# Loading the first two products' weights in units of 1, 1, 2 and 4 tiles, with the x tiles between them, and eight warm-up products in place of ten

## The chip, the cores and the metric

The kernel runs on one core of one Trainium2 chip. The metric is the device time of one execution in microseconds (us). The kernel before takes 1129.25 us, the median of three runs (1127.74 to 1129.56). One further execution was profiled, and all rows below are of that one.

## The reference

`reference()` takes an activation `x` of 512 positions by 1024 channels in fp32 through two blocks. The first has a gated linear recurrence layer ("layer a") and a sliding-window attention layer ("layer b"); the second has two attentions side by side and a squared-ReLU MLP of 4096. What matters here is how it begins:

```python
h = rmsnorm(x, norm_g)                  # a row of 1024 divided by its root mean square, times g
u = h @ w_in                            # 1024 x 3072
xb, gate = u[..., :1536], u[..., 1536:]
xb = causal_depthwise_conv(xb, conv_w, conv_b)
...                                     # r, i: sigmoids of block products of xb; a, b from them
_, hs = lax.associative_scan(_linear_combine, (a, b), axis=1)
y = hs * silu(gate)
return x + y @ w_out                    # 1536 x 1024
```

## The kernel before, in words

Everything is held transposed: channels on the 128 partitions, the 512 positions along the free axis. `x` is 8 tiles of 128x512 (256 KB each), a weight matrix is cut into tiles of 128x128 (64 KB each). One output tile of `h @ w_in` is 128 channels by 512 positions and sums over 8 pairs of a weight tile and an x tile.

fp32 accuracy is reached with three products for each such pair. An operand is split into a high part, rounded to the type fp32r, and a low part, the difference; the products are high*high, high*low and low*high (`mm3`, L443). So each weight that is loaded is first rounded (`hi_task`, L491: an ACT, DVE or POOL instruction) and then subtracted (`lo_task`, L505: always DVE), and each x tile is multiplied by its norm weight and rounded on ACT, and subtracted on DVE (`split`, L647). The division by the root mean square is put off: it is applied when an output leaves PSUM, so the first products don't wait for the norm, only the first evacuations do (`wait_norm`, called in `xb_evac`, L777).

Weights arrive in units, listed in `plan` in the order in which the products use them. A unit is usually 8 tiles (512 KB). The first two outputs are computed together by `gemm_pair` (L580): for each segment of the sum, one unit of output 0 and one of output 1 are taken, and the two outputs' products alternate along k, so that each x tile is used for six products when it comes. In the kernel before a segment there has 4 tiles, so the pair has four units of 256 KB.

Three tasks handle units: `raw_task` (L479) issues the DMA, `hi_task` rounds, `lo_task` subtracts. `raw_task` may run ahead by `RAW_MAX` = 6 widths of 512 columns. `pieces` (L474) says in how many instructions a unit is rounded and subtracted: the first unit in pieces of 128 columns, others whole. `x_load(j)` (L1716) issues the DMA of x tile j; tile 0 follows the small tensor `vec` (93 KB, norm weights and biases), and tile j > 0 waits until more than (j + 1) // 2 units have been issued. All DMAs go through one queue, SP's.

The order of all instructions is not written out by hand. A planner (`Sched`, L100) holds the tasks as generators, keeps a clock for each engine with its own costs, and each time picks the task with the lowest priority number among those that can start within a window on an engine; an operation that may run on several engines goes to the one where it would finish first. It draws random priorities from seeds; for each of four stages of the network eight seeds are tried in the planner and the one with the earliest planned end is taken (`_orders`, L1877). The instructions of the whole kernel come out of this, so a change at the start can reorder what lies behind it. In the rounding step units with an index below 8 may go to ACT or DVE (`also="copy"`), those from 8 on to ACT or POOL (`also="pool"`).

Before the first real product, `WARM` products of a zeroed bf16 tile (L1731) run on PE.

Layer a ends with `a_w_out`: its first four outputs are computed over the gated tiles y_a[0] to y_a[7] first and over y_a[8] to y_a[11] later (`gemm_open`, L605). DVE makes the low part of each y_a tile as the last step of a chain of gate, scan and product (`rg_post`, `ga_evac`).

Of the kernel before, what the change touches and what calls it, by code (L numbers as in the profile page):

```python
# [16 lines left out]
P = 128  # L17
T = 512
# [9 lines left out]
NSM = 48  # L28
RAW_MAX = 6
LOOK = 6  # L30
WARM = 10
MAXU = 6
WINDOW = 40.0
SLACK = 800.0
# [241 lines left out]
def kernel(ctx: ExitStack, tc: tile.TileContext, io: dict, out: bass.AP, seeds=(0,), trial=False):  # L276
# [12 lines left out]
    fa = Slots(NS_F)  # L289
# [21 lines left out]
    def f_(i):  # L311
        return FB[:, i, :]

    def p_(i):
        return PS[:, i, :]
# [105 lines left out]
    def MMS(lst):  # L421


        def emit():
            for o, l, r, st, sp, _ in lst:
                nc.tensor.matmul(out=o, lhsT=l, rhs=r, start=st, stop=sp)  # L426

        dur = 0.0
        rd, wr = [], []
        seen = set()  # L430
        for o, l, r, _, _, c in lst:
            dur += c
            for lst2, ap in ((rd, l), (rd, r), (wr, o)):
                k = (ap.name, ap.offset, tuple(ap.shape))
                if k not in seen:
                    seen.add(k)
                    lst2.append(ap)
        return Op([("PE", dur, emit, None)], rd, wr)
# [4 lines left out]
    def mm3(o, wh, wl, xh, xl, start, stop):  # L443
        c = cost(_free(o))
        return [(o, wh, xh, start, False, c), (o, wh, xl, False, False, c), (o, wl, xh, False, stop, c)]
# [8 lines left out]
    def DMA(o, i):  # L454
        n = _free(o) * o.shape[0] * 4
        return Op([("SP", n / 360.0, lambda: nc.sync.dma_start(out=o, in_=i), None)], [i], [o])  # L456
# [6 lines left out]
    pos = {"u": 0, "s": 0, "r": 0}  # L463

    def wide(i):
        return (plan[i].shape[-1] + T - 1) // T

    def span(a, e):
        return sum(wide(i) for i in range(a, e))
# [3 lines left out]

    def pieces(i):  # L474
        n = plan[i].shape[-1]
        st = P if i == 0 else 2 * T
        return [(c, min(c + st, n)) for c in range(0, n, st)]

    def raw_task():  # L479
        for i in range(len(plan)):  # L480
            w = wide(i)
            yield lambda: i <= pos["s"] or (span(pos["s"], i + 1) <= RAW_MAX and (i < pos["s"] + 2 or fa.room() >= 6))
            s = yield from fa.get(w)
            n = plan[i].shape[-1]
            yield DMA(FBW[:, s * T:s * T + n], plan[i])
            raws[i] = s
            pos["r"] = i + 1
# [3 lines left out]
    def hi_task():  # L491
        for i in range(len(plan)):
            w = wide(i)
            yield lambda: i in raws and (
                i <= pos["u"] or span(pos["u"], i + 1) <= 2 or (span(pos["u"], i + 1) <= LOOK and ra.room() >= 12)
            )
            s = yield from ra.get(2 * w)
            for c, e in pieces(i):
                yield A(
                    RBW[:, s * T + c:s * T + e], FBW[:, raws[i] * T + c:raws[i] * T + e], AF.Copy,  # L500
                    also="copy" if i < 8 else "pool",
                )
            his[i] = s

    def lo_task():  # L505
        for i in range(len(plan)):
            yield lambda: i in his
            w = wide(i)
            s = his.pop(i)
            for c, e in pieces(i):  # L510
                yield TT(
                    RBW[:, (s + w) * T + c:(s + w) * T + e], FBW[:, raws[i] * T + c:raws[i] * T + e],
                    asf(RBW[:, s * T + c:s * T + e]), ALU.subtract,
                )
            fa.free(raws.pop(i), w)
            units[i] = (s, w)
            pos["s"] = i + 1
# [5 lines left out]
    def need():  # L523
        i = pos["u"]
        pos["u"] += 1
        yield lambda: i in units
        return units.pop(i)

    def wpair(u, c):

        s, w = u
        return RBW[:, s * T + c.start:s * T + c.stop], RBW[:, (s + w) * T + c.start:(s + w) * T + c.stop]

    def wfree(u):
        ra.free(u[0], 2 * u[1])
# [3 lines left out]
    def add(u, fn):  # L539
        plan.extend(u)  # L540
        jobs.append(fn)
# [9 lines left out]
    def ksegs(k0, k1, step=8):  # L551
        return [(k, min(k + step, k1)) for k in range(k0, k1, step)]

    def wsl(w, n, a, b):
        return io[w][n, :, a * P:b * P]

    def have(lst, k):
        return lambda: lst[k] is not None
# [19 lines left out]
        add([wsl(w, n, a, e) for a, e in segs], fn)  # L578

    def gemm_pair(w, n0, n1, kt, acts, evac, prio=3):  # L580
        segs = ksegs(0, kt, 4)

        def fn():
            bs = []
            for n in (n0, n1):
                b = yield from pa.get(1, 1)
                bs.append(b)
            for a, e in segs:
                us = []
                for _ in bs:  # L590
                    u = yield from need()
                    us.append(u)
                for k in range(a, e):
                    yield have(acts, k)
                    c = slice((k - a) * P, (k - a + 1) * P)
                    for b, u in zip(bs, us):
                        yield MMS(mm3(p_(b), *wpair(u, c), *acts[k], k == 0, k == kt - 1))
                for u in us:
                    wfree(u)
            for n, b in zip((n0, n1), bs):  # L600
                S.spawn(evac(n, b), prio)

        add([wsl(w, n, a, e) for a, e in segs for n in (n0, n1)], fn)
# [98 lines left out]
    def x_ready(j, gset, nrm):  # L702
        x = f_(xs[j])
        for g, dst in gset:
            S.spawn(split_act(x, g, dst, j), -1 if nrm is n_a else 1)
        S.spawn(sq_add(nrm, x), 4 if nrm is n_a else 1.5)
# [182 lines left out]
    def layer_a():  # L889
# [4 lines left out]
        def ga(a, e):  # L894
            for j in range(a, e):
                gemm("a_w_in", KR + j, KD, act_a, ga_evac)

        gemm_pair("a_w_in", 0, 1, KD, act_a, xb_evac)
        xb(2, 6)
        ga(0,1)  # L900
# [815 lines left out]
    def x_load(j):  # L1716
        if j == 0:
            yield DMA(vec, io["vec"])
        else:
            yield lambda: pos["r"] > (j + 1) // 2  # L1720
        yield DMA(f_(xs[j]), io["x"][j])
        x_ready(j, [("a_g", act_a)], n_a)

    with tc.manual_schedule():
        nc.vector.memset(warm, 0.0)
        nc.vector.memset(eps, EPS)
        nc.vector.memset(half, -0.5)
        nc.scalar.activation(out=lt[:, 0, 0:1], in_=eps, func=AF.Exp)
        S.table = "exp"
        for j in range(WARM):  # L1730
            nc.tensor.matmul(out=p_(7), lhsT=warm[:, 0:P], rhs=warm, start=True, stop=True)  # L1731
        for j in range(KD):
            S.spawn(x_load(j), 0.1 * j)
        S.spawn(raw_task(), 2.5)
        S.spawn(hi_task(), w_prio)
        S.spawn(lo_task(), w_prio)
        S.spawn(const_task(), 0)
        S.spawn(lam_task(), 4)
        S.spawn(main(), 5)
        try:  # L1740
            S.run()
        except Enough:
            return S.clock["PE"]
# [163 lines left out]
```

## Time and profile before

| | before |
|---|---|
| median of three runs | 1129.25 us |
| the profiled execution's own time | 1129.1 us |
| its span in the profile | 1127.3 us |
| mean granted TensorE clock | 0.996 |
| PE busy | 1115.4 us (99%), 5324 instructions |
| DVE busy | 762.4 us (68%) |
| ACT busy | 404.0 us (36%) |
| POOL busy | 269.2 us (24%) |

PE is TensorE's matmul stream, PEld its weight loads, DVE is VectorE, ACT is ScalarE, POOL is GpSimd, SP is SyncE, whose queue (SPq) issues the DMAs. Times in the rows are microseconds from the start of the span. The 1.8 us between the span and the execution's own time lie around the span. A matmul's end is modelled, so PE counts as busy also where products are spaced wider than they could be; the number of products in a stretch tells more than the busy time there.

### The profile page before, as it was taken

How to read it: one execution, taken by the hardware profiler on the slowest of the kernel's cores; microseconds unless marked ns; L12 is line 12 of the kernel's file. 1: busy time of each engine (PE TensorE's matmuls, PEld its weight loads, DVE VectorE, ACT ScalarE, POOL GpSimd, SP SyncE). 2: the span in 40 equal slices, each digit the busy share in tenths (PEclk: the TensorE clock that was granted, in tenths of full speed). 3: DMA queues.
4: the chain of work that ended last, by engine and by line, in shares of the span. 5: the costliest groups of instructions: out<-in, count | busy, mean ns of one | idle time of the engine just before them, and what ended most of it. 6: DMA issues, size and time to landing. Idle time of an engine off the chain costs nothing.

```text
span 1127.3 us, 14746 instructions
## 1 busy us (share of the span) xinstructions
PE 1115.4 (99%) x5324; PEld 931.0 (83%) x5324; DVE 762.4 (68%) x1349; ACT 404.0 (36%) x823; POOL 269.2 (24%) x353
## 2 busy tenths in 40 slices
PE   9999999999999999999999999999999999999997
PEld 6888888888888878888888888888888888888887
DVE  7999999675797896668676477786653235655332
ACT  5447753334767621177153253111111211111111
POOL 1222242023746521043123124213100002111100
PEclk9999999999999999999999999999999999999998
DMA  7334345306333521712554625423333322233001
GB/s 292 90 113 124 116 131 187 97 16 171 108 92 86 176 80 46 220 54 97 166 167 115 188 91 186 169 94 107 99 94 112 113 75 94 75 93 112 1 1 75
DMA packets 46792, 127.41 MB, mean 113 GB/s; under 512 B 6272, under 2 KB 7936, under 8 KB 46720
## 3 DMA queue, kind: packets, MB, share of 16 engines
q1 hardware_dynamic: 46720, 126.47, 35.8%
q8 instruction: 42, 0.69, 0.3%
q14 instruction: 30, 0.25, 0.1%
HBM read 106.53 MB, written 2.10 MB: 96 GB/s over the span
## 4 chain that ended last, share of the span: by engine, by line
PE 93%; DVE 2%; issue 1%; DMA 1%; SPq 1%; POOL 1%; ACT 1%; POOLq 0%; DVEq 0%; ACTq 0%
PE ps L426 90%; PE ps L450 3%; SPq L456 1%; DMA fb<-in_mk 1%; DMA fb<-in_a_w_in 0%; DVE rb L374 0%; ACT rb L350 0%; DVE fb L374 0%; POOL fb L402 0%; DVE fb L994 0%; POOL col_b L416 0%; DVE fb L405 0%; DVE rb L388 0%; ACT fb L350 0%; DVE fb L388 0%
## 5 line engine op out<-in xcount | busy, mean ns | idle before, releaser
L426 PE MATMUL ps<-rb 128*128 128x512 f32 (+2 forms) x4856 | 1083.6, 382 | 3.0 <-ACT rb L350 2.5
L426 PEld LDWEIGHTS ps<-rb 128*128 128x128 f32 x4856 | 877.2, 188 | 173.6 <-ACT rb L350 3.6
L374 DVE TENSOR_TENSOR rb<-fb,rb 128x1024 fp32r<-128x1024 f32 (+5 forms) x305 | 297.3, 995 | 69.4 <-ACT rb L350 58.0
L359 POOL TENSOR_SCALAR rb<-fb 128x1024 fp32r<-128x1024 f32 (+4 forms) x149 | 156.9, 1062 | 611.6 <-PE ps L426 479.9
L350 ACT ACTIVATE rb<-fb 128x512 fp32r<-128x512 f32 (+4 forms) x149 | 109.2, 741 | 357.1 <-DVE fb L388 164.2
L374 DVE TENSOR_TENSOR fb<-ps,fb 128x512 f32<-128x512 f32 (+3 forms) x142 | 83.5, 590 | 138.4 <-PE ps L426 123.1
L374 DVE TENSOR_TENSOR fb<-fb 128x512 f32<-128x512 f32 (+1 forms) x120 | 88.1, 740 | 23.2 <-ACT rb L350 21.3
L402 POOL TENSOR_SCALAR fb<-fb,sm 128x256 f32<-128x256 f32 (+2 forms) x112 | 64.8, 595 | 118.4 <-DVE sm L419 76.9
L350 ACT ACTIVATE fb<-fb,sm 128x256 f32<-128x256 f32 (+2 forms) x128 | 65.3, 513 | 37.1 <-DVE sm L396 23.2
L388 DVE SCALAR_TENSOR_TENSOR fb<-ps,fb 128x512 f32<-128x512 f32 x56 | 38.5, 687 | 55.4 <-PE ps L426 55.3
L350 ACT ACTIVATE rb<-ps 128x512 fp32r<-128x512 f32 (+2 forms) x86 | 45.3, 537 | 77.3 <-PE ps L450 67.9
L374 DVE TENSOR_TENSOR rb<-ps,rb 128x512 fp32r<-128x512 f32 (+2 forms) x86 | 51.9, 612 | 28.3 <-ACT rb L350 26.6
L350 ACT ACTIVATE fb<-fb 128x512 f32<-128x512 f32 (+1 forms) x63 | 37.5, 611 | 62.0 <-DVE fb L374 54.3
L350 ACT ACTIVATE rb<-fb,vec 128x512 fp32r<-128x512 f32 x41 | 28.5, 719 | 85.3 <-DVE fb L374 74.8
L350 ACT ACTIVATE fb<-ps 64x256 f32<-64x256 f32 (+2 forms) x68 | 30.0, 442 | 63.9 <-PE ps L426 31.5
L450 PE MATMUL ps<-ident,fb 128*128 128x128 f32 x328 | 49.8, 272 | 1.2 <-DVE fb L1593 0.9
L450 PEld LDWEIGHTS ps<-ident,fb 128*128 128x128 f32 x328 | 40.6, 140 | 11.3 <-DVE fb L1593 1.1
L994 DVE CUSTOM_DVE_ANT_0 fb<-ps,fb 128x256 f32<-128x256 f32 (+1 forms) x64 | 28.8, 487 | 11.4 <-PE ps L426 9.5
L388 DVE SCALAR_TENSOR_TENSOR rb<-fb,vec,rb 128x512 fp32r<-128x512 f32 x41 | 30.5, 762 | 0.3
L388 DVE SCALAR_TENSOR_TENSOR fb<-fb,vec 128x512 f32<-128x512 f32 x36 | 29.1, 829 | 0.0
L994 DVE CUSTOM_DVE_ANT_0 fb<-ps,fb,sm_qs 128x256 f32<-128x256 f32 (+1 forms) x64 | 26.3, 442 | 2.7 <-POOL fb L402 1.3
L350 ACT ACTIVATION_READ_ACCUMULATOR fb<-fb,sm 128x1 f32 x128 | 24.1, 189 | 0.0
(90 smaller groups left out, 331.3 us busy)
## 6 DMA issues: line engine op xcount, KB each, us to landing
rb<-rb SPq DMA_DIRECT2D x128, 128.0 KB, 2.3
fb<-in_w_down SPq DMA_DIRECT2D x32, 512.0 KB, 3.7
fb<-in_w_in SPq DMA_DIRECT2D x31, 512.0 KB, 4.1
fb<-in_w_up SPq DMA_DIRECT2D x29, 512.0 KB, 3.5
fb<-in_a_w_in SPq DMA_DIRECT2D x22, 512.0 KB, 4.1
fb<-in_b_w_in SPq DMA_DIRECT2D x16, 512.0 KB, 3.7
fb<-in_mb SPq DMA_DIRECT2D x8, 640.0 KB, 4.6
fb<-in_a_w_out SPq DMA_DIRECT2D x8, 512.0 KB, 3.5
```

The lines of the kernel that those rows point to most:

```text
L350: opts = [("ACT", dur, lambda: nc.scalar.activation(out=o, in_=i, func=fn, **kw), TABLES.get(fn))]
L359: lambda: nc.gpsimd.tensor_scalar(out=o, in0=i, scalar1=1.0, scalar2=1.0, op0=ALU.mult, op1=ALU.mult), None,
L374: lambda: nc.vector.tensor_tensor(out=o, in0=a, in1=b, op=op), None,
L388: lambda: nc.vector.scalar_tensor_tensor(out=o, in0=a, scalar=s, in1=b, op0=op0, op1=op1), None,
L402: ("POOL", 262.0 + 0.832 * n, lambda: nc.gpsimd.tensor_scalar(out=o, in0=a, scalar1=s, scalar2=1.0, op0=ALU.mult, op1=ALU.mult), None),
L426: nc.tensor.matmul(out=o, lhsT=l, rhs=r, start=st, stop=sp)
L450: nc.tensor.transpose(o, i, ident)
L456: return Op([("SP", n / 360.0, lambda: nc.sync.dma_start(out=o, in_=i), None)], [i], [o])
L994: nc.vector.tensor_tensor_reduce(out=pt[h], in0=PS[:, b, o0:o0 + nk], in1=m, scale=sc, scalar=-3.0e38, op0=ALU.add, op1=ALU.max, accum_out ...
```

## The change

Three edits. The pair's segments become 1, 1, 2 and 4 tiles long, which gives eight units (64, 64, 64, 64, 128, 128, 256 and 256 KB) in place of four of 256 KB, each rounded and subtracted in one instruction. The x tiles are issued at other points between the units, and the first ten units may be issued however far `raw_task` is ahead. The number of warm-up products falls from ten to eight.

```diff
-WARM = 10
+WARM = 8
...
     def pieces(i):
         n = plan[i].shape[-1]
-        st = P if i == 0 else 2 * T
-        return [(c, min(c + st, n)) for c in range(0, n, st)]
+        return [(0, n)]
...
-            yield lambda: i <= pos["s"] or (span(pos["s"], i + 1) <= RAW_MAX and (i < pos["s"] + 2 or fa.room() >= 6))
+            yield lambda: i < 10 or i <= pos["s"] or (span(pos["s"], i + 1) <= RAW_MAX and (i < pos["s"] + 2 or fa.room() >= 6))
...
     def gemm_pair(w, n0, n1, kt, acts, evac, prio=3):
-        segs = ksegs(0, kt, 4)
+        segs = [(0, 1), (1, 2), (2, 4), (4, kt)]
...
         else:
-            yield lambda: pos["r"] > (j + 1) // 2
+            yield lambda: pos["r"] >= (0, 2, 4, 6, 6, 8, 8, 8)[j]
         yield DMA(f_(xs[j]), io["x"][j])
```

## Rows read from the trace of the kernel before

**Rows 1.** The page, part 1: busy us, share of the span, instructions of each engine.
```profile
PE 1115.4 (99%) x5324; PEld 931.0 (83%) x5324; DVE 762.4 (68%) x1349; ACT 404.0 (36%) x823; POOL 269.2 (24%) x353
```

**Rows 2.** Timeline of PE, 0 to 60 us: start, us, engine, line, tiles, count.
```profile
1.17 4.35 PE L1731 MATMUL ps<-warm 128*128 128x512 bf16 x10 [1.17 <-DVE half L1727]
5.12 1.30 PE L426 MATMUL ps<-rb 128*128 128x512 f32 x3
7.91 17.13 PE L426 MATMUL ps<-rb 128*128 128x512 f32 x66 [1.49 <-ACT rb L350]
24.88 0.95 PE L426 MATMUL ps<-ones,fb 128*128 128x1 f32 x8
```

**Rows 3.** Windows of 1 us, PE: length, busy (products), PEclk, DMA share, GB/s.
```profile
8.00:9.00 1.00, 1.00 (x3) 0.85 1.04 397
9.00:10.00 1.00, 1.00 (x3) 0.50 1.07 412
...
12.00:13.00 1.00, 1.00 (x5) 0.94 1.00 399
```

**Rows 4.** Timeline of SP's queue, first eight microseconds, five of its issues.
```profile
0.72 0.38 SPq L456 DMA_DIRECT2D vec<-in_vec  x1
1.16 0.42 SPq L456 DMA_DIRECT2D fb<-in_x  x1
1.62 0.43 SPq L456 DMA_DIRECT2D fb<-in_a_w_in  x1
2.10 0.43 SPq L456 DMA_DIRECT2D fb<-in_a_w_in  x1
...
7.22 0.33 SPq L456 DMA_DIRECT2D fb<-in_x  x1
```

**Rows 5.** DMA issues, those five in order: count, KB, us from issue to landing.
```profile
vec<-in_vec SPq DMA_DIRECT2D x1, 93.0 KB, 2.0
fb<-in_x SPq DMA_DIRECT2D x1, 256.0 KB, 2.6
fb<-in_a_w_in SPq DMA_DIRECT2D x1, 256.0 KB, 3.1
fb<-in_a_w_in SPq DMA_DIRECT2D x1, 256.0 KB, 5.1
...
fb<-in_x SPq DMA_DIRECT2D x1, 256.0 KB, 5.1
```

**Rows 6.** Timeline of ACT, 3 to 20 us, the rounding of x tiles 1 and 2.
```profile
7.85 1.34 ACT L350 ACTIVATE rb<-fb,vec 128x512 fp32r<-128x512 f32 x2
```

**Rows 7.** Timeline of DVE, 3 to 30 us.
```profile
7.88 0.69 DVE L374 TENSOR_TENSOR rb<-fb,rb 128x512 fp32r<-128x512 f32 x1 [1.44 <-ACT rb L350]
8.61 1.41 DVE L388 SCALAR_TENSOR_TENSOR rb<-fb,vec,rb 128x512 fp32r<-128x512 f32 x2
...
13.99 0.68 DVE L354 CAST rb<-fb 128x1024 fp32r<-128x1024 f32 x1
...
29.81 0.69 DVE L374 TENSOR_TENSOR fb<-ps,fb 128x512 f32<-128x512 f32 x1 [3.39 <-ACT fb L350]
```

**Rows 8.** Window of layer a: busy us (count) of PE, PEld, DVE, ACT, POOL.
```profile
30.00:190.00 160.00, 160.00 (x706) 131.95 (x705) 159.62 (x221) 90.94 (x132) 43.10 (x35) 1.00 0.42 128
```

**Rows 9.** Timelines of PE from 160 us and of DVE from 186 us.
```profile
159.82 77.91 PE L426 MATMUL ps<-rb 128*128 128x512 f32 x343
...
191.13 2.02 DVE L374 TENSOR_TENSOR rb<-fb,rb 128x512 fp32r<-128x512 f32 x2
193.57 0.69 DVE L374 TENSOR_TENSOR fb<-ps,fb 128x512 f32<-128x512 f32 x1 [0.41 <-PE ps L426]
```

**Rows 10.** Timeline, 160 to 202 us: one DVE instruction beside POOL and one alone.
```profile
164.90 2.28 POOL L359 TENSOR_SCALAR rb<-fb 128x512 fp32r<-128x512 f32 x2 [0.28 <-DMA fb<-in_a_w_out]
165.08 1.62 DVE L374 TENSOR_TENSOR rb<-fb,rb 128x1024 fp32r<-128x1024 f32 x1
...
171.06 1.21 DVE L374 TENSOR_TENSOR rb<-fb,rb 128x1024 fp32r<-128x1024 f32 x1
```

## The prediction

> **What bounds the kernel now.** I read the page's busy times first: PE is busy 1115.4 of 1127.3 us [rows 1], so the kernel is bound by its products, and a change at the start can win only what PE loses there, and only if nothing later takes it back. So the next views are the start on PE, then the transfers that feed it, then the engine that is nearest to being a second bound.
>
> PE's timeline shows ten warm-up products, three real ones from 5.12, a wait of 1.49, and from 7.91 on 66 products without idle time [rows 2]. Without idle time doesn't mean at full pace: a long stretch of the same products takes 77.91 us for 343, that is 0.227 each [rows 9]. Count back from the next thing PE does: at 24.88 it has done 69 real products, so at full pace it would have started at 24.88 - 69 x 0.227 = 9.22. I call this the equivalent start. Two things make 9.22 out of 5.12. One is the wait for output 1's first unit: it is issued at 2.10 and lands 5.1 later, at 7.2 [rows 4, 5], and its rounding and the product follow. The other is the clock: after that wait the granted clock is 0.85 from 8 to 9, 0.50 from 9 (the first of three such rows) and 0.94 from 12 to 13 [rows 3], so it was at its lower level of 1.2 GHz for 0.3 + 3 + 0.12 = 3.4 us. There 512 columns take 0.427 (the ten warm-up products fit that: 4.35 us), so the loss is 3.4 x (1 - 0.227/0.427) = 1.6.
>
> A check of this account: product 8 is the first that needs the low part of x tile 1. That tile is rounded from 7.85 [rows 6] and its low part is done by 8.61 + 0.7 = 9.3 [rows 7]; 9.3 less seven products is 7.7, plus 1.6 for the clock is 9.3, against 9.22 seen.
>
> The second bound is DVE. From 30 to 190 us it is busy 159.62 of 160 [rows 8]. Its last work for y_a[11] is one of two subtractions that run from 191.13 to 193.15, and then it waits for PE, 0.41, to evacuate the first output that used it [rows 9]. So at 193 the two engines meet within a few tenths. A PE that comes there earlier will wait for DVE, unless DVE comes earlier as well.
>
> **The smaller units and the new order of x.** The landing times of before give a curve of bytes: 93 KB at 0.72 + 2.0 = 2.7, 349 at 1.16 + 2.6 = 3.8, 605 at 1.62 + 3.1 = 4.7, 861 at 7.2, and the transfer issued at 7.22 at 12.3 [rows 4, 5]. Eight transfers of 256 KB land after 7.2 up to that one, 0.64 each (410 GB/s). I take the same curve with the new order, interpolated in bytes: x0 3.8, units of one tile 4.0 and 4.25, x1 5.95, the next two 6.6 and 7.2, x2 7.85, two-tile units 8.2 and 8.5, x3 9.1, x4 9.8, four-tile units 10.4 and 11.0, x5 to x7 11.7, 12.3, 13.0. An x tile's low part is there 0.7 (ACT) and 0.75 (DVE) later [rows 6, 7]. The equivalent start that each asks for is that time less the products before it: x1, 7.5 - 7 x 0.227 = 5.9; x2, 9.35 - 13 x 0.227 = 6.4; x3, 10.6 - 19 x 0.227 = 6.3; x4 5.6; x5 6.1; x7 4.7; the four-tile units 5.6 to 6.0. The latest is 6.4, and I add 0.1 for queues on ACT and DVE: 6.5. Against 9.22 PE gains 2.7 if the clock stays up, and 2.7 - 1.6 = 1.1 if it falls again as before. Will it? Before, PE did three products and then waited 1.49. Now it has six from about 4.9, the wait for x1 is some 0.6 long, and the next six follow. I take it that it stays.
>
> Bounds: the curve's slow piece (2.5 us for 256 KB between 4.7 and 7.2) may fall elsewhere. Without it, at 0.64 throughout, x2 lands 1.9 earlier and the start would be near 4.9 (gain 4.3, where the first product then bounds). If a small unit takes as much of the queue as a large one, the gain is nothing (below).
>
> Sync's queue has 17 issues for vec, x and the pair in place of 13, and two more units may be issued early. At some 0.43 to 0.46 each [rows 4] four more are 1.8 us, but already before the x tile at 7.22 was issued only when an earlier transfer had landed at 7.2, so issuing isn't what ends last; I take 0, up to 0.5 if the small ones leave the queue empty. The instructions of a unit: four more roundings and subtractions of 128 to 256 columns in place of four of 128 and two larger; I take 0.3 more on DVE.
>
> **Eight warm-ups.** Two fewer at 0.427 end at 1.17 + 8 x 0.427 = 4.6 in place of 5.4. The first real product can't start before x0 is rounded, at about 4.5, and its weight, about 4.8. So nothing is won on PE but a queue that is free in time, and the cost is 0 unless the gap lets the clock stay low; then the first six products take 1.2 longer, of which the wait for x1 hides some half: 0.6 at most.
>
> **What reaches the end.** DVE waits 1.44 until 7.88 for output 1's rounding [rows 7]. With x1 at 5.95 its low part starts near 6.7, 1.1 earlier. The rounding of 128x1024 at 13.99, 0.68 [rows 7], belongs to a unit with a new index of 8 or more, which no longer may go to DVE: 0.7 more, less the 0.3 above. DVE is then ahead by 1.5. Its wait of 3.39 for the norm, which ends at 29.81 [rows 7], I leave as it is: what ends it is a chain of small steps on three engines. So of PE's 2.7 only 1.5 passes 193 us for sure. The rest would need DVE relieved by a better plan. I take 1.8, between 1.5 and 2.7 but near the row. What lies behind is planned anew; PE's idle time there has no row that a change at the start would remove, and I take 0, with 1.5 either way for a different order.
>
> The sum is made against the profiled execution: 1129.1 - 1.8 = 1127.3. The median of the runs is 0.15 above it, so I give 1127.4.
>
> **Rivals.**
> *Everything arrives.* DVE's work is shared out otherwise (ACT is busy 90.94 of those 160 us [rows 8]) and the whole 2.7 to 4.3 comes through: 1125 to 1126.5. For it: the planner may move roundings and squares to ACT. Against: subtractions, most of DVE's work, can't move.
>
> *The clock falls again.* PE gains 1.1: 1128.1. For it: the wait for x1 is only shortened. Against: there are more products around it.
>
> *Small units cost what large ones do.* Then the n-th transfer lands as the n-th landed before, whatever its size. In the curve x3, now the eleventh, lands at 11.7 and asks for 13.2 - 4.3 = 8.9; the gain is 0.3 and the time 1128.9. For it: vec, 93 KB, still needs 2.0 from issue to landing where 256 KB need 2.6 [rows 5]. Against: the 256 KB behind vec land 1.0 later, and most of the 2.0 may overlap. The Trainium skill speaks for this rival in DMA: Bandwidth & Descriptors, section Bandwidth: batch a DMA to 1 MiB or more; it lists 64 KB at 0.95 us of transfer, so four such units would be 3.8 us, an estimate from that page, where the curve has four times 0.25 at its early pace. The trace shows 1.0 between vec and x0, and no transfer of 64 KB from memory, so it decides neither way.
>
> *DVE falls behind: slower.* The units with index 4 to 7 of before (outputs 2 to 5, each of 128x1024) now have index 8 and up, so their roundings go to ACT or POOL. A DVE subtraction of 128x1024 takes 1.62 beside POOL and 1.21 alone [rows 10]. ACT is full in that stretch with x tiles and squares, so all four may go to POOL, where one runs beside two DVE instructions: 8 x 0.41 = 3.3, and if a plan with more work on POOL goes on through layer a, another eight such meetings are 3.3 more. From 1.5 + 2.3 = 3.8 on the kernel is slower by over 0.2%; the whole 6.6 gives 1129.1 - 1.5 + 6.6 = 1134, and a middle of 4.5 gives 1132. Against: DVE is no worse off by one rounding that leaves it.
>
> **How the numbers follow.** About 0.2% (2.3 us) is what a measurement of this kernel can tell from no change, so faster means below 1127.0 and slower above 1131.5. My forecast has 0.36, of which 0.13 lies below 1127.0 because PE's gain of 2.7 is larger than what I let through. Everything arrives has 0.27, the clock 0.13, small units 0.10, DVE behind 0.14. Faster is 0.27 + 0.13 = 0.40; slower 0.14; the same 0.23 + 0.13 + 0.10 = 0.46. The forecast alone lies within 1126.0 to 1128.9. The range of 8 in 10 starts where all of 4.3 arrives (1124.8) and ends at 1131.0, which leaves out most of the slower case.
>
> **What would show it.** The landing of x1 near 6 and of x2 near 7.9; 69 products done 2.7 earlier, so an equivalent start near 6.5; a granted clock of 1.00 from 6 us on; DVE's first evacuation (29.81 before) 1 to 2 earlier; and at the end of layer a a wait of PE for DVE of about 1 us, where before there was none. The prediction is wrong if the equivalent start moves less than 1 or more than 4, if PE doesn't wait for DVE near 190 us and the whole gain stays, or if PE's idle time behind layer a changes by more than 1.5.

## The result, and the profile after

The changed kernel takes 1135.51 us, the median of four runs (1135.10 to 1138.12), against 1128.72 for the kernel before in four runs of its own: a ratio of 1.0065, with a 95% interval of 1.0047 to 1.0083. The forecast was 1127.4 and a range up to 1131.0; the kernel became 6.8 us slower. The profiled execution is the slowest of the four (1138.12, span 1136.3), so some 2.6 us of what its trace shows are not typical.

PE's wait and DVE's order are to be read together. First the timeline of PE from 0 to 27 us, which answers to [rows 2] (start, us, engine, line, tiles, count; in brackets the idle time before it and what ended it; line numbers from 477 on are one lower than before):

```profile
1.17 3.42 PE L1730 MATMUL ps<-warm 128*128 128x512 bf16 x8 [1.17 <-DVE half L1726]
...
5.49 1.65 PE L426 MATMUL ps<-rb 128*128 128x512 f32 x6 [0.19 <-DVE rb L388]
...
9.30 1.77 PE L426 MATMUL ps<-rb 128*128 128x512 f32 x6 [0.29 <-DVE rb L388]
...
17.19 9.63 PE L426 MATMUL ps<-rb 128*128 128x512 f32 x34 [2.00 <-DVE rb L374]
26.66 0.94 PE L426 MATMUL ps<-ones,fb 128*128 128x1 f32 x8
```

Product 18, counting from 0, starts at 10.68: an equivalent start of 10.68 - 18 x 0.227 = 6.59, where 6.5 was forecast. Then it is lost. Products 19 to 28 come in small groups (8.44 at product 28), and product 29 waits 2.00 for DVE. The 34 products from 17.19 need 9.6 us, where 34 x 0.227 = 7.7 would be full pace: the clock has fallen. The windows of 1 us on PE (busy, products, granted clock, DMA share, GB/s):

```profile
17.00:18.00 1.00, 0.81 (x3) 0.97 1.03 422
18.00:19.00 1.00, 1.00 (x4) 0.50 1.04 426
19.00:20.00 1.00, 1.00 (x4) 0.50 1.00 407
```

The same 0.50 as in [rows 3], 1.2 GHz, comes later and after another wait. At 26.66, 63 products are done, so the equivalent start is 26.66 - 63 x 0.227 = 12.36: 3.1 later than the 9.22 of before, not 2.7 earlier.

What PE waited for is on DVE's timeline from 13 to 18 us:

```profile
13.48 0.69 DVE L374 TENSOR_TENSOR rb<-fb,rb 128x512 fp32r<-128x512 f32 x1
14.37 0.75 DVE L388 SCALAR_TENSOR_TENSOR rb<-fb,vec,rb 128x512 fp32r<-128x512 f32 x1 [0.21 <-ACT rb L350]
15.04 0.17 DVE L388 SCALAR_TENSOR_TENSOR lt<-vec 128x12 f32<-128x12 f32 x1
15.12 1.41 DVE L388 SCALAR_TENSOR_TENSOR rb<-fb,vec,rb 128x512 fp32r<-128x512 f32 x2
16.45 0.68 DVE L374 TENSOR_TENSOR rb<-fb,rb 128x512 fp32r<-128x512 f32 x1
17.05 0.69 DVE L374 TENSOR_TENSOR fb<-fb 128x512 f32<-128x512 f32 x1
```

At 13.48 stands the low part of output 0's four-tile unit, at 16.45 that of output 1's. Between them are the low parts of x5, x6 and x7 (L388), which are needed later than that, from product 30 on. The planner gives an x tile's split a lower priority number than a weight's low part, so it goes first. PE goes on 0.06 after 17.13, where the subtraction ends.

The rest of the 8.8 us by which this trace is late is found by comparing the two traces at the same amount of work (all products counted, 0.227 for each of 512 columns): 3.1 at 20 us of work, 2.9 at 120, 5.4 at 140, 4.2 at 300, 6.2 at 320, 8.4 at 400, 8.8 at the end. The jumps lie at waits; here are PE's waits (us in total, times, the longest):

```profile
PE ps L426 <- ACT rb L350: 2.9, 2, 2.5
PE ps L426 <- DVE rb L374: 2.7, 3, 2.0
PE ps L426 <- DMA rb<-rb: 2.4, 1, 2.4
PE ps L450 <- POOL fb L402: 1.2, 1, 1.2
```

The 2.4 ends at 141.98 and the 2.5 at 409.47. The first is named DMA, but the chain of waits that leads to it (start, us, what) is almost all DVE until the copy is issued; the copy itself lands 4.79 later:

```profile
132.52 1.45 DVE fb L374
133.97 0.87 DVE rb L374
134.84 0.60 DVE fb L388
135.44 0.07 DVE rb L374
135.51 0.46 issue
135.97 0.69 DVE rb L374
136.66 0.02 issue
136.67 0.33 SPq L456
137.01 0.04 issue
137.05 4.79 DMA rb<-rb
```

The window from 30 to 190 us, against [rows 8] (busy us and count of PE, PEld, DVE, ACT, POOL; clock, DMA share, GB/s):

```profile
30.00:190.00 160.00, 157.56 (x698) 130.20 (x697) 157.84 (x213) 90.01 (x130) 48.66 (x37) 1.00 0.41 126
```

PE does 698 products where it did 706. POOL is busy 48.66 where it was 43.10, but not because the four roundings of the slower rival moved to it: of those with a new index of 8 to 11 ACT does three and POOL one (18.84 to 20.43), and up to 190 us POOL rounds 24 units of 128x1024 where it rounded 23. They take longer, 1.52 on the mean in place of 1.27.

What does change on DVE is its start into layer a. Its first evacuation comes at 34.05, where it came at 29.81 [rows 7], and DVE doesn't wait before it. In front of it stand the steps that compute small constants of 128x12 (`lam_task`), which start when more than six units have been asked for. With four more units in the pair that is earlier: they were done by 61.6 us before, and are by 34.2 now. Four of them run beside a row of POOL roundings and take 0.76 to 0.98 each, each ending 0.01 to 0.03 after a POOL instruction; in an experiment below, the one with POOL emptied, six of the same steps take 1.19 together with no POOL rounding beside them. DVE in the changed kernel, POOL in the changed kernel, and DVE in that experiment:

```profile
29.78 3.61 DVE L388 SCALAR_TENSOR_TENSOR lt<-lt 128x12 f32<-128x12 f32 x4
...
34.05 1.88 DVE L374 TENSOR_TENSOR fb<-ps,fb 128x512 f32<-128x512 f32 x3
```

```profile
28.90 4.47 POOL L359 TENSOR_SCALAR rb<-fb 128x768 fp32r<-128x768 f32 x4
```

```profile
27.52 1.19 DVE L388 SCALAR_TENSOR_TENSOR lt<-lt 128x12 f32<-128x12 f32 x6
```

Behind the wait at 409 the clock falls once more, to 0.50 from 410.5 on (a window of PE):

```profile
411.00:412.00 1.00, 1.00 (x4) 0.50 0.87 152
```

### The profile page after: what moved, and what is told of

Its sections match the earlier page's. It is cut to its first block, busy times and chain, and to the rows that moved or that the text cites. A ratio compares the mean times of both kernels' runs of the same rounds, so it can differ in the third digit from the quotient of the medians.

```text
span 1136.3 us, 14740 instructions
## 1 busy us (share of the span) xinstructions
PE 1117.1 (98%) x5322; PEld 931.7 (82%) x5322; DVE 759.3 (67%) x1347; ACT 401.0 (35%) x822; POOL 283.0 (25%) x358
## 4 chain that ended last, share of the span: by engine, by line
PE 85%; DVE 9%; issue 3%; POOL 1%; DMA 1%; SPq 1%; ACT 0%; DVEq 0%; POOLq 0%
PE ps L426 82%; PE ps L450 3%; DVE fb L388 3%; DVE rb L374 2%; DVE fb L374 2%; DVE fb L861 1%; POOL fb L402 1%; SPq L456 1%; DMA fb<-in_x 1%; DMA rb<-rb 0%; DVE lt L388 0%; POOL sm_qs L416 0%; DVE rb L354 0%; POOL sm_qt L412 0%; ACT rb L350 0%
## 5 line engine op out<-in xcount | busy, mean ns | idle before, releaser
L374 DVE TENSOR_TENSOR rb<-fb,rb 128x1024 fp32r<-128x1024 f32 (+5 forms) x306 | 290.3, 970 | 64.4 <-ACT rb L350 53.5
L359 POOL TENSOR_SCALAR rb<-fb 128x1024 fp32r<-128x1024 f32 (+5 forms) x157 | 174.4, 1120 | 628.1 <-PE ps L426 464.3
L350 ACT ACTIVATE rb<-fb 128x512 fp32r<-128x512 f32 (+4 forms) x138 | 100.9, 737 | 323.8 <-DVE fb L388 152.6
L402 POOL TENSOR_SCALAR fb<-fb,sm 128x256 f32<-128x256 f32 (+2 forms) x106 | 59.0, 573 | 108.7 <-DVE sm L419 70.8
L388 DVE SCALAR_TENSOR_TENSOR fb<-ps,fb 128x512 f32<-128x512 f32 x56 | 38.5, 687 | 59.7 <-PE ps L426 59.7
L993 DVE CUSTOM_DVE_ANT_0 fb<-ps,fb 128x384 f32<-128x384 f32 (+1 forms) x64 | 29.2, 485 | 11.0 <-PE ps L426 7.8
L388 DVE SCALAR_TENSOR_TENSOR rb<-fb,vec,rb 128x512 fp32r<-128x512 f32 x41 | 30.7, 762 | 2.2 <-ACT rb L350 1.8
L388 DVE SCALAR_TENSOR_TENSOR fb<-fb,vec 128x512 f32<-128x512 f32 x36 | 32.1, 914 | 0.0
L388 DVE SCALAR_TENSOR_TENSOR fb<-fb 128x512 f32<-128x512 f32 x32 | 24.3, 767 | 0.4 <-ACT fb L350 0.3
```

The lines of the kernel that those rows point to most:

```text
L350: opts = [("ACT", dur, lambda: nc.scalar.activation(out=o, in_=i, func=fn, **kw), TABLES.get(fn))]
L359: lambda: nc.gpsimd.tensor_scalar(out=o, in0=i, scalar1=1.0, scalar2=1.0, op0=ALU.mult, op1=ALU.mult), None,
L374: lambda: nc.vector.tensor_tensor(out=o, in0=a, in1=b, op=op), None,
L388: lambda: nc.vector.scalar_tensor_tensor(out=o, in0=a, scalar=s, in1=b, op0=op0, op1=op1), None,
L402: ("POOL", 262.0 + 0.832 * n, lambda: nc.gpsimd.tensor_scalar(out=o, in0=a, scalar1=s, scalar2=1.0, op0=ALU.mult, op1=ALU.mult), None),
L993: nc.vector.tensor_tensor_reduce(out=pt[h], in0=PS[:, b, o0:o0 + nk], in1=m, scale=sc, scalar=-3.0e38, op0=ALU.add, op1=ALU.max, accum_out ...
```

## The experiments

All times are medians; ratios are to the kernel before, run beside it on the same chip, with 95% intervals. "Late" and "early" are against the trace of before at the same amount of work.

**Eight warm-ups alone.** The kernel before with one edit:

```diff
-WARM = 10
+WARM = 8
```

> The kernel before with eight warm-up products in place of ten and nothing else; the order of all other instructions is that of the kernel before. Theory A (the loss comes from the order of VectorE's work in the pair and from the new plan behind it): the equivalent start stays at 9.2 within 0.4 and the time at 1128.7 within 1. Rival (eight warm-ups leave the clock low): the first real products are 0.43 apart from 5.1 on, the equivalent start is 0.6 to 1.6 later, 1129.3 to 1130.3.

1128.21, ratio 0.9997 [0.9988, 1.0006]: nothing, as forecast. The first products still lie wide apart (three take 1.79, and from 8.4 to 10.1 they are 0.427 apart, the spacing at 1.2 GHz), though the granted clock reads 1.00 in each of these windows; from 10.4 on they are 0.23 apart, and the equivalent start was 8.7. So this trace is 0.5 early from the head on. It stays so through layer a, with no wait, though DVE is busy 159.62 of the 160 us there as before: DVE's first evacuation is 0.49 earlier, too (29.81 before), since the chain that ends DVE's wait for the norm passes through four transposes on PE, which begin at 28.05 (28.55 before) though their input was there at 27.4 (27.6): PE comes to them earlier. The last row is DVE's.

```profile
5.53 1.79 PE L426 MATMUL ps<-rb 128*128 128x512 f32 x3 [0.76 <-ACT rb L350]
7.77 16.77 PE L426 MATMUL ps<-rb 128*128 128x512 f32 x66 [0.45 <-ACT rb L350]
```

```profile
29.32 1.89 DVE L374 TENSOR_TENSOR fb<-ps,fb 128x512 f32<-128x512 f32 x3 [3.04 <-ACT fb L350]
```

**The wait at product 29 taken away.** In the changed kernel the low parts of the two four-tile units go ahead of everything on DVE, and their rounding stays on ACT:

```diff
-                    also="copy" if i < 8 else "pool",
+                    also=None if i in (6, 7) else "copy" if i < 8 else "pool",
...
-        S.spawn(lo_task(), w_prio)
+        S.spawn(lo_task(), lambda: -2.0 if pos["s"] in (6, 7) else w_prio())
```

> The changed kernel, but the low parts of the pair's two four-tile units go ahead of the x tiles on VectorE, and their roundings to ScalarE alone. Theory A: the wait of 2.0 before product 29 goes, and with it the fall of the clock at 18 us; the equivalent start, 12.4 in the changed kernel, becomes 8.5 to 9.0. Rival B (late landing of the transfers bounds the pair, the order on VectorE hardly matters): the equivalent start stays above 10.5. The time is open by about 3 us either way since the plan behind is a new one: A 1129 to 1134, B 1133 to 1137.

1137.32, ratio 1.0078 [1.0066, 1.0091]: not faster at all, and above both ranges that were expected. Yet the head did what it was meant to. From product 11 on PE runs without a wait; 72 products are done at 24.44, and product 60 starts at 21.56, which gives 21.56 - 60 x 0.227 = 7.94. The trace is 1.27 early at 10 us of work and 0.76 at 20. A row of PE's timeline, and its waits:

```profile
10.34 14.11 PE L426 MATMUL ps<-rb 128*128 128x512 f32 x61 [1.66 <-DVE rb L374]
```

```profile
PE ps L426 <- DVE rb L374: 4.6, 3, 2.7
PE ps L426 <- DMA rb<-rb: 4.5, 2, 3.1
PE ps L426 <- DVE rb L354: 2.2, 1, 2.2
```

It gives that back in layer a: 3.7 late at 60 us of work, 8.4 at 140, 8.6 at the end. The waits lie at 48, 53 and 139, and after the last one, 3.13 long, the clock is low. So the wait at the head is one fault, and what lies behind it is another, larger one.

**The clock kept up through that wait.** Nine products of the zeroed tile, whose result nobody reads, are put into PE's stream ahead of product 29 (in the trace they stand before product 27, two products ahead of the wait):

```diff
+    def filled(emit):
+        def both():
+            for _ in range(FILL):
+                nc.tensor.matmul(out=p_(7), lhsT=warm[:, 0:P], rhs=warm, start=True, stop=True)
+            emit()
```

> The changed kernel, with nine products of the zeroed warm-up tile put into TensorE's stream just before product 29, where it waits 2.0; no other instruction moves. Theory A, as to the clock: the clock doesn't fall, the equivalent start is 10.7 in place of 12.4. If VectorE is the second bound in layer a (theory D), the 1.6 are given back at the wait near 139 us, which grows by as much, and the time stays at 1135 to 1136; if it isn't, the time is 1133 to 1134.

1137.02 (1134.08 to 1139.45), ratio 1.0075 [1.0063, 1.0087]: no gain in time. At the head the clock stayed up:

```profile
18.00:19.00 1.00, 1.00 (x6) 1.00 1.05 430
```

The equivalent start was 10.32 in place of 12.36: product 29 started 0.41 earlier, and 1.6 are the clock (3.4 us at the lower level). That the filling kept the clock up is not shown by this one trace. Five traces have the wait at product 29 unfilled: after 2.00 (changed kernel), 2.14 (the same again) and 2.26 us (seeds 16 to 23) the clock fell to 0.50; after 1.97 (unit numbers moved) and 2.25 (ACT alone, old order) it stayed at 1.00. Behind the head this run has the same waits, near 138, 326 and 404, and ends 7.1 late. The wait near 138 did not grow by what the head gained, as was expected if DVE takes it back; it was 1.35 where it had been 2.44.

**Other plans of both kernels.** The planner tries eight random seeds for each stage. The same kernels with the next seeds, and the ones after those:

```diff
-        for seed in range(ORDERS):
+        for seed in range(8, 8 + ORDERS):
```

(and `range(16, 16 + ORDERS)`). The changed kernel with seeds 8 to 15:

> The changed kernel, with the planner's candidates 8 to 15 in place of 0 to 7: another order by the same rules. Theory P (what the kernel loses behind the pair, 5.6 us in waits near 139, 328 and 406 us, is the luck of one plan): the waits sit elsewhere and the time moves by 2 to 6 us, most likely down, 1129 to 1134. Rival (the loss behind the pair belongs to the change): the same waits come back and the time is 1134 to 1137.

the kernel before with seeds 8 to 15:

> The kernel before with the planner's candidates 8 to 15. Theory P (a new plan costs several us, with or without the change): PE waits appear behind the pair that the shown plan hasn't, and the time is 1130 to 1136. Rival (the loss behind the pair belongs to the change, plans of the kernel before are all as dense): within 1.5 of 1128.3. The equivalent start is 9.2 within 0.7 in both, since the pair's order hardly hangs on the seeds.

the kernel before with seeds 16 to 23:

> The kernel before with the planner's candidates 16 to 23, a third plan of it. Theory P: 1130 to 1136. Rival: within 1.5 of 1128.3.

the changed kernel with seeds 16 to 23:

> The changed kernel with the planner's candidates 16 to 23, a third plan of it. Theory P: 1130 to 1137, and the mean over three plans is that of the kernel before over its three plus the change at the head (equivalent start 10.7 to 12.4 against 9.2), so 1.5 to 3 more. Rival (the change costs more behind the pair in every plan): the mean over the plans lies 5 or more above.

and the changed kernel once more as it was:

> The changed kernel once more, for its spread and a second profile. The order of its instructions is fixed, so the waits before product 29, near 139, 328 and 406 us come again and the time is 1135 to 1138; what may differ between executions is whether the clock falls after a wait (1.6 us each time), so its runs spread by about 3 us where those of the kernel before spread by 2.

| seeds | kernel before | changed kernel |
|---|---|---|
| 0 to 7 | 1128.32 | 1135.51; again 1136.86, ratio 1.0068 [1.0052, 1.0084] |
| 8 to 15 | 1132.76, 1.0041 [1.0028, 1.0053] | 1131.89, 1.0038 [1.0024, 1.0052] |
| 16 to 23 | 1130.42, 1.0014 [1.0005, 1.0023] | 1138.21, 1.0089 [1.0062, 1.0116] |

The same program moves by 4.4 us with its plan, and the plan shown as the kernel before is the best of its three. By these three plans some 2 of the 6.8 us are its luck: the means are 1130.5 and 1135.2. With seeds 8 to 15 the two kernels are the same. With three plans each, the mean difference of 4.7 is not measured well; it lies between what was expected of the luck of plans (1.5 to 3) and of a loss in every plan (5 or more). The changed kernel run again has a second trace (1137.22) with the same waits: 2.14 at product 29, 2.12 near 141, 1.19 near 329, 2.49 near 409. It is 2.6 late at 20 us of work, 4.5 at 140, 5.3 at 320, 7.5 at 380 and 7.9 at the end; its runs spread over 6 us where 3 was expected. And one thing is alike in every plan of the changed kernel: PE stops for about 2 us just before product 29, or in the products ahead of it. In seeds 16 to 23 (first row) it is the same subtraction; with seeds 8 to 15 (the other three) 1.50 falls ahead of product 27 and 0.53 ahead of 29:

```profile
16.43 10.29 PE L426 MATMUL ps<-rb 128*128 128x512 f32 x37 [2.26 <-DVE rb L374]
```

```profile
12.23 2.13 PE L426 MATMUL ps<-rb 128*128 128x512 f32 x8 [0.17 <-DVE rb L388]
15.86 0.73 PE L426 MATMUL ps<-rb 128*128 128x512 f32 x2 [1.50 <-DVE rb L354]
17.13 8.68 PE L426 MATMUL ps<-rb 128*128 128x512 f32 x37 [0.53 <-DVE rb L374]
```

The kernel before has a wait of the kind that the changed kernel has at 139, near 50, in both of its other plans: 1.89 with seeds 16 to 23, and with seeds 8 to 15

```profile
52.61 3.65 PE L426 MATMUL ps<-rb 128*128 128x512 f32 x8 [1.92 <-DMA rb<-rb]
```

**DVE made lighter.** The kernel of the second experiment with two of the four taps of the convolution left out, which takes 24 instructions of 128x512 from DVE:

```diff
-        for k in (2, 1, 0):
+        for k in (2,):
```

> The kernel of e2_w_first with two of the four taps of the convolution left out, which takes 24 VectorE instructions of 128x512, some 17 us, from layer a and nothing from TensorE. Theory D (VectorE is the second bound of layer a and takes back what the head gains): the waits of TensorE near 48, 53 and 139 us, 9.7 in all behind the pair in e2_w_first by 140 us, go, and at 240 us TensorE is still ahead of the kernel before by about the 1.3 of the head. Rival (the waits come from the order, not from VectorE's load): over 3 us of waits stay before 240 us.

1126.97, ratio 0.9982 [0.9972, 0.9991]. There is no wait in layer a any more: the 1.4 by which it is early at 10 us of work is 1.4 at 180 and 2.5 at the end. DVE is busy 148.44 of the 160 us.

```profile
30.00:190.00 160.00, 159.79 (x708) 132.01 (x707) 148.44 (x193) 93.20 (x131) 50.73 (x38) 1.00 0.44 140
```

So the head's gain comes through with less work on DVE. This is a new plan, too, and as work is left out, it is a test and no proposal.

**POOL emptied instead, with all of the work done.** Units 6 to 37 are rounded by ACT alone, the low parts in the order of the second experiment:

```diff
-                    also="copy" if i < 8 else "pool",
+                    also="copy" if i < 6 else None if i < 38 else "pool",
```

> The kernel of e2_w_first, with all weight roundings of layer a's input products (units 6 to 37) on ScalarE alone in place of ScalarE or GpSimd: a VectorE subtraction of 128x1024 takes 1.62 beside a GpSimd rounding and 1.21 alone, and there are 22 of them in layer a, so VectorE is relieved by up to 8 us with nothing left out. Theory D (VectorE's load takes back the head's gain): no wait of over 1 us before 240 us, TensorE 1 or more ahead of the kernel before there, and the time 1126 to 1130 as the plan behind falls. Rival (the order decides, not the load): waits of 3 us and more near 50 and 139 us stay, 1131 to 1138.

1128.15 (1126.56 to 1131.36), ratio 0.9995 [0.9986, 1.0004]. Equivalent start 7.34, no wait in layer a, 2.8 early at the end of the profiled run, which is the fastest of the twelve. By the medians nothing is gained: 1127.99 is that of the kernel before beside it. The window from 30 to 190 us:

```profile
30.00:190.00 160.00, 160.00 (x707) 132.32 (x706) 150.23 (x211) 108.22 (x149) 16.25 (x13) 1.00 0.44 134
```

Against the second experiment POOL's 54.64 went to 16.25, ACT's 90.39 to 108.22, and DVE, with about as many instructions, was busy 150.23 in place of 155.96 while PE did 41 products more. DVE does the same subtractions and gets through them sooner when POOL is quiet, as [rows 10] had it for one instruction: those of 128x1024 take 1.28 on the mean in this window, where they took 1.36 in the second experiment.

Three kernels are its controls. The kernel before with eight warm-ups, seeds 8 to 15 and units 4 to 33 on ACT alone:

> The kernel before with eight warm-ups, the same relief of VectorE (units 4 to 33 rounded on ScalarE alone), and candidates 8 to 15: how much of e10 is the relief without the change. Theory D: no gain in layer a, as TensorE has no wait there in the kernel before; 1127 to 1132 by the luck of the plan. If it is as fast as e10, the smaller units are worth nothing even when VectorE is relieved.

1128.94, 1.0006 [0.9997, 1.0014], against 1132.76 for these seeds without the edits: the wait near 50 is gone here too, and the equivalent start is 7.9. This experiment's kernel with seeds 16 to 23:

> The kernel of e10 with the planner's candidates 16 to 23, a second plan of it. Theory D: again no wait of over 1 us before 240 us, TensorE ahead of the kernel before by 1 or more there; behind it the luck of the plan, 1126 to 1131. Rival: waits of 3 us and more in layer a come back.

1129.89, 1.0010 [1.0002, 1.0019]; and with seeds 8 to 15:

> The kernel of e10 with the planner's candidates 8 to 15, a third plan of the mended order with VectorE relieved. Theory D: no wait of over 1 us before 240 us, TensorE ahead by 1 or more there, 1126 to 1131. Whether the version beats the kernel before is open: its first two plans gave 1128.2 and 1129.9 against 1128.0.

1128.63, 0.9997 [0.9987, 1.0006], with no wait of over 1 us in layer a, but only 0.7 early at 240 us of work, as its equivalent start is 9.3. Over its three plans the kernel with POOL emptied has 1128.9 on the mean, where the kernel before has 1130.5 and the changed one 1135.2. Against the one plan of before that is shown as the kernel before, it is the same. So it is against the kernel before with ACT alone, which was expected to tell what the smaller units are worth: 1128.94 there, 1128.63 here with the same seeds, with intervals that overlap. No run with all of the work done shows a gain of the smaller units.

**The unit numbers moved along.** The slower rival said that a unit's higher number sends its rounding to POOL. In the changed kernel the limits move with the four extra units:

```diff
-                    also="copy" if i < 8 else "pool",
+                    also="copy" if i < 12 else "pool",
...
-        yield lambda: pos["u"] > 6
+        yield lambda: pos["u"] > 10
```

> The changed kernel with the two conditions on a unit's number moved along with the pair's four more units: roundings may go to VectorE up to unit 11 (7 in the changed kernel), and the small constants (lam_task) start after ten units (six in the changed kernel). Theory I (the shifted numbers load VectorE and bring the loss of layer a): no wait of over 1 us between 30 and 240 us; the wait before product 29 stays, since the order of low parts there is as it was; 1131 to 1134. Rival D (the load of VectorE by all of layer a's work, of which the shift is a small part): waits of 2 to 4 us stay in layer a, 1133 to 1138.

1130.45, ratio 1.0011 [1.0001, 1.0020]. The wait at product 29 stays (first row), and the trace is 2.0 late from there on. But layer a has no wait, though DVE is busy 159.06 of the 160 us (second row: 707 products, POOL 43.73), and the trace ends 0.8 late. The small constants are computed from 34 us on, and DVE's first evacuation comes at 30.43; up to 190 us POOL rounds 20 units of 128x1024, not 24.

```profile
16.95 8.00 PE L426 MATMUL ps<-rb 128*128 128x512 f32 x34 [1.97 <-DVE rb L374]
```

```profile
30.00:190.00 160.00, 160.00 (x707) 132.48 (x707) 159.06 (x224) 95.23 (x136) 43.73 (x33) 1.00 0.42 132
```

With the numbers moved, 5 of the 6.8 us are gone. Two numbers were moved at once and the plan is a new one, so it isn't shown which of the three brought the 5. In the two traces, 1.1 of the difference is at the head, where the clock stayed up, 2.7 at 139, and the rest behind layer a.

**ACT alone without the new order of low parts.** The changed kernel with units 8 to 37 rounded by ACT alone:

```diff
-                    also="copy" if i < 8 else "pool",
+                    also="copy" if i < 8 else None if i < 38 else "pool",
```

> The changed kernel with the relief of VectorE alone (units 8 to 37 rounded on ScalarE only), and the order in the pair as in the changed kernel. Theory D with theory A: the wait before product 29 stays, with an equivalent start of 10.3 to 12.4, and layer a has no wait of over 1 us behind it; TensorE is 1 to 3 behind the kernel before at 240 us, where the changed kernel is 4.2 to 5.1 behind; 1129 to 1134 with the luck behind. Rival: waits in layer a stay.

1135.07, ratio 1.0058 [1.0039, 1.0078], above the 1129 to 1134 expected. The wait at product 29 is there (2.25), layer a has none, and at 372 us of work the trace is 0.8 early. Then PE waits 3.23 and 1.62 at 401 to 406, and the clock is at 0.50 from 404.9 to 411.7 (the row of PE, and two windows):

```profile
404.03 0.50 PE L426 MATMUL ps<-rb 128*128 128x512 f32 x1 [3.23 <-ACT rb L350]
```

```profile
404.00:405.00 1.00, 0.50 (x1) 0.93 0.00 0
405.00:406.00 1.00, 0.00 (x0) 0.50 0.00 0
```

It is 5.3 late from there to the end. So the loss of this kernel lies at one place, far behind the change, in a stage whose code the change doesn't touch. The kernel before waits for the same product, but less:

```profile
402.64 0.50 PE L426 MATMUL ps<-rb 128*128 128x512 f32 x1 [1.01 <-ACT rb L350]
```

The chain that ends last is of one kind in all three traces: behind a product ACT and DVE take small steps in turn, each waiting for the one before. It takes 5.8 us in the kernel before (from 397.56), 9.1 in the changed kernel (from 401.11) and 6.9 here (from 399.23), and PE has other products for the first 4.1, 5.9 and 1.6 us of it. In the changed kernel the chain is longer by a weight unit's subtraction that stands in it at 402.86 and takes 2.09 beside POOL (the kernel before has it at 396.40, ahead of the chain, and 1.23). Here nothing of the kind stands in it; PE has run out of other products, and the clock adds to it. That the two plans put things so is seen; what in the change makes them do so is open, and the place was not tried by itself.

## Why the prediction was wrong

**What was right.** PE's bound, the reading of the head by the equivalent start, the landings to x2 (x1 5.77 against 5.95, x2 7.71 against 7.85) and the start at product 18, 6.59 against 6.5. The warm-ups cost 0, and the clock stayed up through the wait for x1. *Small units cost what large ones do* fell: x3, the eleventh transfer, landed at 9.60, where that rival had 11.7; the curve had 9.1. The 64 KB units landed 0.2 to 0.6 after the transfer ahead of them. One reading was wrong there: the trace of before does have transfers of 64 KB from memory. Two pairs of them, issued 0.38 apart near 677 and 683 us, land 0.65 and 0.62 apart, which is what 256 KB took in the curve; this row spoke for the rival.

```profile
fb<-in_w_pb SPq DMA_DIRECT2D x4, 64.0 KB, 1.9
```

**The step that failed first: "I add 0.1 for queues on ACT and DVE".** The latest tile was taken to set the start, and each low part to be there 0.75 after its tile. In the order of DVE's instructions the low part of output 1's four-tile unit stood behind those of three x tiles: the equivalent start of 8.44 at product 28 became 10.61 at product 29. I had worked out that 0.3 more DVE work was added and not in which order it would be done. Behind the wait the clock fell, 12.36, which the forecast had as a rival with 1.6, at another place. The third experiment has the head without that fall (10.32), the second without the wait (7.94).

**The curve of bytes was too early behind x2.** x4 landed at 11.69 where 9.8 was forecast, the four-tile units at 12.34 and 12.95 where 10.4 and 11.0 were, as between 8 and 10 us the queue moved 243 and 193 GB/s, where [rows 3] has 397 and 412. With the order mended the equivalent start was 7.3 to 8.3, not 6.5, and 9.3 in one plan. On the mean that is 8.1 over five kernels, against 8.7 for the kernel before, its other plans and eight warm-ups (9.2, 9.2, 8.7, 8.5, 7.9): at the head the smaller units are worth about half a us, less than either group spreads.

**"So of PE's 2.7 only 1.5 passes 193 us" had a full engine, but not the way in which it costs.** The wait for the norm was left as it was; with eight warm-ups alone PE and DVE's first evacuation both came 0.5 earlier, and the 0.5 passed 193 us with DVE busy 159.62 of 160. In the changed kernel the evacuation, forecast 1 to 2 before 29.81, came at 34.05, as the small constants that are started by a unit's number moved ahead of it and ran beside POOL. The prediction doesn't have that second condition on a unit's number. There was no wait at 193; there was one of 2.4 near 139, and in the second experiment there were 2.7, 1.4 and 3.1 near 48, 53 and 139. The seven traces of the changed kernel in which the first evacuation comes at 33.0 to 34.1 are those without relief of POOL and with the numbers as they were; six of them have a wait in layer a, and the seventh has less work on DVE. In the five other kernels with the change it comes at 29.4 to 31.2 and none has a wait of over 1 us there. That fits a DVE that starts late and has no slack, but two plans of the kernel before have a wait near 50 with an evacuation at 29.1 and 30.5, so it isn't the only cause. The rival *DVE falls behind* had the right engine and, in the total, nearly the right time (1132 to 1134), by another way: one of its four roundings went to POOL, not all, and its 6.6 in layer a were 2.4 at 139. That is luck more than mechanism.

**"What lies behind is planned anew; ... and I take 0, with 1.5 either way" was mis-sized.** Three plans of one program, the kernel before, lie 4.4 us apart, and the place near 400 alone cost 3.1 in the changed kernel and 6.2 in the last experiment. With these plans known, the plan of before is the best of its three, and its successor could be expected to lose, not to break even: the term would be about +2 with 3 either way. The prediction had the one plan of the kernel before to go by.

Together, in the profiled run: 3.1 at the head in place of -2.7, 2.5 at 139, then -1.2 up to 300 us of work, +2.0 near 320 (1.2 of it the wait for POOL), +3.1 near 400, and small differences, 8.8 in all. The median run is 2.6 below this one; which of the terms is smaller in it is not shown, as it has no trace.

Not settled: how much of the 139-us wait is the constants' early start, how much the roundings and how much the plan's luck, and why the plans differ near 400. No version tried is shown to beat the kernel before with all of the work done; the best, 0.9995 and 0.9997, can't be told from it.

## What to carry to other kernels

When a load is cut into smaller pieces, follow each piece through the engine that prepares it, in the order of that engine's queue: the piece that lands in time is of no use behind others that are needed later. Look for every condition that counts the pieces: here one of them started other work on the fullest engine earlier. A busy share of 159.6 of 160 doesn't tell by itself whether a gain at the head is lost (0.5 passed with it); what tells is whether that engine's work comes earlier, too. With POOL's roundings moved to ACT the same products left it busy 150.2. Where a planner makes the order, run two or three plans of both kernels before a difference below half a percent is put down to the change.

## What the runs showed of the hardware

The granted clock fell to 0.50 after waits of 2.0 to 3.2 us: in the changed kernel at 18 and at 410, in the second experiment at 142, in the last at 405. At the last three places PE had run for 75 us and more without a wait of 0.8 us. It stayed there for 3.4 us in the first three cases and for 6.8 in the last. It isn't so after every such wait: in the changed kernel's own trace the wait of 2.44 that ends at 141.98 is followed by a clock of 1.00, in the second experiment that of 2.70 at 51 is, and with the numbers moved along the wait of 1.97 at product 29 is followed by 34 products in 8.00, where in the changed kernel 34 took 9.63. That may be a part of why one program's runs lie apart (1133.6 to 1139.7 for the changed kernel run again); it was not tried, and the kernel before, whose longest wait behind the head is 1.0, has runs from 1127.3 to 1132.3.

A DVE instruction beside POOL roundings can take several times its time alone: 0.76 to 0.98 us for a step of 128x12 that takes 0.17 alone, each ending with a POOL instruction in the changed kernel at 30.6 to 33.4.

The queue starts slowly: 193 to 302 GB/s from 5 to 10 us in the changed kernel, and 407 to 426 from 15 to 21 us, with transfers of 64 to 256 KB first and mostly larger ones later. In the kernel before it is 219 to 279 from 5 to 8 us and 397 to 412 from 8 to 10, and the kernel with POOL emptied, which issues the same first transfers as the changed one, has 353 and 369 from 8 to 10. What ends the slow stretch is not shown.
